# A decoder block on one core: the accounts of the last experts and the final sums

## The chip, the cores and the metric

One core of one Trainium2 chip. The metric is the device time of one execution in microseconds (us); the times given are medians of several runs. The engines are named as in the profile: PE is TensorE, ACT ScalarE, DVE VectorE, POOL GpSimd, SP SyncE (here it only issues DMAs). DMAs issued by SP are made by hardware; the indirect ones that gather and scatter rows by index are issued by GpSimd, which writes their descriptors itself.

## The reference

A decoder block on 512 tokens of 1024 channels in float32: a Mamba-2 mixer and a pooling mixer, merged; then a mixture of 64 experts (256 hidden channels each, 8 of them for each token) and one shared expert; then a final norm. The change lies in the last part:

```python
u2 = modulate(rmsnorm(h, norm_ffn_g), sh2, sc2)
h = h + g2 * moe_ffn(u2, ...)      # routed experts, each weighted, plus the shared expert
return rmsnorm(h, final_norm_g)    # h * rsqrt(mean(h*h) + eps) * g
```

## The kernel before

Tokens lie in four tiles of 128 partitions by 1024 channels (`NT` = 4, `t` counts them). The mixers come first; this document only needs the loop over experts in `experts` and the function `finish`.

The experts run one after the other, in an order written out by hand (`manual_schedule`). For expert `e` the kernel gathers its tokens' rows (a gather on GpSimd), multiplies them by the gate and up weights, forms the hidden product, and multiplies by the down weights. Experts of up to 64 tokens take a light way through PE in float32; others a heavy one, in which ACT and DVE split each weight tile into two parts first. The iteration of `e` runs the down product of `e - 1`, and then the scatter of `e - 1`: GpSimd adds the weighted output rows into one of two accounts in DRAM, `Y[0]` or `Y[1]` (512 x 1024 each, an accumulating indirect DMA). Before the change even experts go to `Y[0]` and odd ones to `Y[1]`, so that two scatters that follow each other need not wait for each other; scatters into the same account do. `Y[0]` starts as the shared expert's output and `Y[1]` as zeros. The number of rows in a scatter is chosen by Ifs on the expert's count (`first`); tokens over 128 go in a second one (`second`). An If's other arm counts up the semaphores that its DMAs would have counted.

Weights come by DMAs on SP's queue, in order, into a ring of eight tiles of 128 x 2048 named `raw`, three for each expert; a load waits until the tile's last reader is done. Behind the last expert's weights SP loads, into tiles of the same ring, the residual `hs2` (two pairs of token tiles, `L1324`), the two rows `k.rows` (the gate g2 and the final norm's weights, broadcast to all partitions, `L1093`, `L1094`), and then `part`, the two pairs of token tiles of `Y[0]` (`L1324` again; both use `token_pair`). For the last expert (63, heavy) the down product and its scatter stand behind the loop. Behind them `part` is multiplied by g2 (`L1290`) and added to `hs2` (`L1291`), tiles 0 and 2 on DVE, 1 and 3 on GpSimd.

`rare_blocks` is an If that is not taken here (an expert with over 256 tokens). `finish` reads the four tiles of `Y[1]` into the tiles of `part` (`L1350`, variable `acc`), multiplies by g2 (`L1345`), adds the sum of before (`L1346`; tile 1 on GpSimd, the others on DVE), squares on ACT with a sum over the row (`L1336`), forms the inverse root on GpSimd in two operations on 128 x 1 (`rsqrt_mean`, `L68` and `L69`), multiplies by the norm's weights on DVE (`L1340`), scales by the root on ACT (`L1341`) and stores (`L1342`).

Of the kernel before, what the change touches and what calls it, by code (L numbers as in the profile page):

```python
# [16 lines left out]
ALU = mybir.AluOpType  # L17
# [6 lines left out]
NT = 4  # L24
# [1018 lines left out]
def scatter(k, idx, b, y, acc, n=P):  # L1043
    k.nc.gpsimd.indirect_dma_start(out=k.Y[acc], out_offset=bass.IndirectOffsetOnAxis(ap=idx[0][:n, b:b + 1], axis=0), in_=y[:n],  # L1044
                                   in_offset=None, bounds_check=T - 1, oob_is_err=False, compute_op=ALU.add)
# [29 lines left out]
def experts(k, shared):  # L1075
# [35 lines left out]
    def sized(n, rows, move):  # L1111
# [6 lines left out]
        with some.Else():  # L1118
            sized(n, rows[mid:], move)

    def first(e, move):
        sized(count(e), (16, 32, 48, 64, 80, 96, 112, P), move)

# [106 lines left out]
    with tc.manual_schedule():  # L1230
        fetch_over(0)
        fetch_over(1)
        if_two(0, lambda: turn(k, k.xg[3], k.xT[1]))
        for e in range(E):
            fetch(e + 2)
            fetch_over(e + 2)
            onehot(e + 4)
            for i in (e, e + 1):
                if i < E:
                    for engines in (every, both):  # L1240
                        count(i, engines)
            if_heavy(e + 1, both, lambda: gu[e + 1][0].split(k, k.gu0w[(e + 1) % 2]))
            hid = products(e)
            hid1, halves = hidden(k), turn_tiles(k)
            slots = slot_tile(k, 2) if e + 4 < E else None

            def turns():
                if e + 1 < E:
                    turn_in(k, xg[e + 1], halves)

            def second_products():
                gate_act(k, gate_up_mm(k, k.xT[(e + 1) % 2], gu[e]), hid1)
                turns()

            def index_part(b):
                if e + 4 < E:
                    slot_product(k, slots, oh[e + 4], k.V[:, :, e + 4, :], b)

            def next_second():
                index_part(0)  # L1260
                turn(k, k.xg[3 + (e + 1) % 2], k.xT[e % 2])

            def second_down():
                ps = turn_tiles(k)[0].rearrange("p q t -> p (q t)")[:, :2 * P].rearrange("p (j t) -> p j t", j=2)
                hidden_in(k, hid1, ps)
                index_part(1)
                hidden_out(k, ps, k.hx[2])
                for n in range(2):
                    down(k, k.hx[2], dn[e], n, k.xg[2], idx[e][1][:, 1:2])

            if_two(e, second_products, turns)
            turned(e + 1, halves)
            if_two(e + 1, next_second, lambda: index_part(0))
            downs(e - 1)
            hidden_turned(e, hid)
            if_two(e, second_down, lambda: index_part(1))
            if e > 0:
                first(e - 1, lambda n: scatter(k, idx[e - 1], 0, k.yl[(e - 1) % 2], (e - 1) % 2, n))
            second(e, lambda n: scatter(k, idx[e], 1, k.xg[2], e % 2, n))
            load(e + 2)  # L1280
            if e + 4 < E:
                idx[e + 4] = slot_numbers(k, slots, 2)
        e = E - 1
        downs(e)
        first(e, lambda n: scatter(k, idx[e], 0, k.yl[e % 2], 1, n))
        part = k.part = [token_pair(k, k.Y[0], t) for t in (0, 2)]
        for t in range(NT):
            eng = (nc.vector, nc.gpsimd)[t % 2]
            y, h = (u[t // 2][:, t % 2, :] for u in (part, k.hs2))
            eng.tensor_mul(y, y, k.rows[:, 0, :])  # L1290
            eng.tensor_add(h, h, y)  # L1291


def rare_blocks(k):
# [33 lines left out]
def finish(k, out):  # L1328
    nc = k.nc
    ys = k.part  # L1330
    ss = k.wp.tile([P, NT], F32, name="oss")
    inv = k.wp.tile([P, NT], F32, name="oinv")
    acc = [ys[t // 2][:, t % 2, :] for t in range(NT)]

    def square(t):
        nc.scalar.activation(k.xg[t], acc[t], AF.Square, accum_out=ss[:, t:t + 1])  # L1336
        rsqrt_mean(k, inv[:, t:t + 1], ss[:, t:t + 1], D)

    def store(t):
        nc.vector.tensor_mul(acc[t], acc[t], k.rows[:, 1, :])  # L1340
        nc.scalar.activation(k.xg[t], acc[t], AF.Copy, scale=inv[:, t:t + 1])  # L1341
        nc.sync.dma_start(out[0, t * P:(t + 1) * P, :], k.xg[t])  # L1342

    def scaled(t, eng):
        eng.tensor_mul(acc[t], acc[t], k.rows[:, 0, :])  # L1345
        eng.tensor_add(acc[t], acc[t], k.hs2[t // 2][:, t % 2, :])  # L1346

    with k.tc.manual_schedule():
        for t in range(NT):
            nc.sync.dma_start(acc[t], k.Y[1][t * P:(t + 1) * P, :])  # L1350
        scaled(0, nc.vector)
        scaled(1, nc.gpsimd)
        square(0)
        scaled(2, nc.vector)
        square(2)
        store(0)
        scaled(3, nc.vector)
        square(1)
        square(3)
        for t in (2, 1, 3):  # L1360
            store(t)


@with_exitstack
# [110 lines left out]
```

## Time and profile before

| | |
|---|---|
| median of 3 runs | 1675.88 us (1669.54 to 1677.01) |
| profiled execution | 1673.0 us |
| its span | 1671.3 us |
| busy: PE, DVE, ACT, POOL | 1475.4, 1011.8, 745.2, 370.3 us |
| last output of expert 63 written by ACT | at 1627.7 us |
| last store issued | at 1663.5 us |

The profile is one execution; its times are us from the start of the span. A row of a timeline gives the start, the duration, the engine, the line of the kernel and the operation as output<-inputs, and in brackets how long the engine was idle before it and what ended that. The engines run side by side, so busy shares don't add up; what counts for the end is the chain of work that ended last. Numbers behind tile names are left out: `raw` can be any tile of the ring.

### The profile page before, as it was taken

How to read it: one execution, taken by the hardware profiler on the slowest of the kernel's cores; microseconds unless marked ns; L12 is line 12 of the kernel's file. 1: busy time of each engine (PE TensorE's matmuls, PEld its weight loads, DVE VectorE, ACT ScalarE, POOL GpSimd, SP SyncE). 2: the span in 40 equal slices, each digit the busy share in tenths (PEclk: the TensorE clock that was granted, in tenths of full speed). 3: DMA queues.
4: the chain of work that ended last, by engine and by line, in shares of the span. 5: the costliest groups of instructions: out<-in, count | busy, mean ns of one | idle time of the engine just before them, and what ended most of it. 6: DMA issues, size and time to landing. Idle time of an engine off the chain costs nothing. (4 is left out here: it accounts for less than half of the span.)

```text
span 1671.3 us, 25992 instructions
## 1 busy us (share of the span) xinstructions
PE 1475.4 (88%) x8084; PEld 1156.2 (69%) x8084; DVE 1011.8 (61%) x1744; ACT 745.2 (45%) x1027; POOL 370.3 (22%) x312
## 2 busy tenths in 40 slices
PE   5999999999999999999898888898798888887970
PEld 5888788788888778888675666566576665665640
DVE  6889778778877974558743354545436453355326
ACT  3465546454434223325544455444536454355332
POOL 5201101002010111220122322322324222221226
PEclk7999999999999999999999999899899989898995
DMA  9442433243333236236738778958889999898974
GB/s 288 122 126 76 138 102 121 76 126 101 107 105 117 82 114 233 87 115 227 294 113 285 252 235 289 329 189 258 282 251 313 324 329 318 287 325 273 297 288 151
DMA packets 152127, 340.32 MB, mean 204 GB/s; under 512 B 15816, under 2 KB 94832, under 8 KB 142272
## 3 DMA queue, kind: packets, MB, share of 16 engines
q1 hardware_dynamic: 135888, 294.94, 51.8%
q0 software_dynamic: 15408, 40.23, 9.4%
q8 instruction: 118, 1.93, 0.5%
q10 hardware_dynamic: 576, 2.10, 0.3%
q14 instruction: 137, 1.12, 0.2%
HBM read 314.00 MB, written 31.01 MB: 206 GB/s over the span
## 5 line engine op out<-in xcount | busy, mean ns | idle before, releaser
L46 DVE TENSOR_TENSOR wl<-raw,wh 128x2048 fp32r<-128x2048 f32 x114 | 273.5, 2404 | 100.0 <-ACT wh L45 88.4
L45 ACT CAST wh<-raw 128x2048 fp32r<-128x2048 f32 x114 | 216.6, 1906 | 140.3 <-PE mm L62 65.7
L1044 POOL DMA_INDIRECT Y<-yl,idx x64 | 108.2, 1691 | 481.8 <-ACT yl L988 271.9
L61 PE MATMUL mm<-uh,wh 128*128 128x512 f32 x432 | 171.7, 397 | 1.9 <-ACT zs L285 1.9
L63 PE MATMUL mm<-uh,wl 128*128 128x512 f32 x432 | 170.4, 395 | 0.0
L62 PE MATMUL mm<-ul,wh 128*128 128x512 f32 x432 | 169.8, 393 | 0.0
L899 PE MATMUL xt<-ident,xg 128*128 128x128 f32 x632 | 97.2, 300 | 58.2 <-issue 18.6
L899 PEld LDWEIGHTS xt<-ident,xg 128*128 128x128 f32 x632 | 84.9, 196 | 77.7 <-issue 48.9
L976 PE MATMUL gu<-raw,xf 128*64 128x256 f32 x1056 | 125.9, 387 | 6.1 <-DMA raw<-in_we_up_dram 3.5
L885 POOL DMA_INDIRECT xg<-u2d,idx x75 | 93.5, 1247 | 117.5 <-DVE oh L851 36.4
L46 DVE TENSOR_TENSOR pair<-raw,pair 128x2048 fp32r<-128x2048 f32 x33 | 75.0, 2290 | 58.2 <-ACT pair L45 49.7
L976 PEld LDWEIGHTS gu<-raw,xf 128*64 128x64 f32 x1056 | 77.2, 138 | 42.6 <-issue 7.2
L61 PE MATMUL gu<-wh,xh 128*128 128x512 f32 x256 | 103.1, 403 | 1.0 <-ACT xh L909 0.6
L62 PE MATMUL gu<-wl,xh 128*128 128x512 f32 x256 | 101.9, 398 | 0.7 <-DVEq L1169 0.7
L63 PE MATMUL gu<-wh,xl 128*128 128x512 f32 x256 | 101.3, 396 | 0.0
L1226 DVE TENSOR_TENSOR hT<-hT,ht 128x128 f32<-128x128 f32 x33 | 9.5, 288 | 146.8 <-ACTq L1169 142.5
L61 PEld LDWEIGHTS mm<-uh,wh 128*128 128x128 f32 x432 | 81.6, 189 | 20.4 <-ACT zs L285 2.3
L63 PEld LDWEIGHTS mm<-uh,wl 128*128 128x128 f32 x432 | 81.6, 189 | 17.7 <-issue 0.9
L62 PEld LDWEIGHTS mm<-ul,wh 128*128 128x128 f32 x432 | 81.5, 189 | 16.8 <-issue 0.4
L45 ACT CAST pair<-raw 128x2048 fp32r<-128x2048 f32 x33 | 62.1, 1903 | 61.7 <-DMA raw<-in_we_gate_dram 22.8
L985 PE MATMUL yo<-raw,hT 128*64 128x512 f32 x264 | 75.5, 695 | 3.5 <-DMA raw<-in_we_gate_dram 2.0
L327 DVE SCALAR_TENSOR_TENSOR cv<-mm,cw,cv 128x511 f32<-128x511 f32 (+2 forms) x90 | 66.6, 741 | 2.1 <-ACT cv L324 1.8
(354 smaller groups left out, 3336.8 us busy)
## 6 DMA issues: line engine op xcount, KB each, us to landing
raw<-in_we_gate_dram SPq DMA_DIRECT2D x124, 512.0 KB
raw<-in_we_up_dram SPq DMA_DIRECT2D x124, 512.0 KB
raw<-in_we_down_dram SPq DMA_DIRECT2D x62, 1024.0 KB
raw<-in_w_in_dram SPq DMA_DIRECT2D x27, 1024.0 KB
raw<-in_w_ada_dram SPq DMA_DIRECT2D x16, 1024.0 KB
big<-in_w_ada_dram SPq DMA_DIRECT2D x16, 512.0 KB
raw<-in_w_in_dram SPq DMA_DIRECT2D x16, 512.0 KB
raw<-in_w_br_ssd_dram SPq DMA_DIRECT2D x8, 1024.0 KB
```

The lines of the kernel that those rows point to most:

```text
L45: nc.scalar.copy(h, raw)
L46: nc.vector.tensor_sub(l, raw, h.bitcast(F32))
L61: nc.tensor.matmul(out, sh, mh, start=first, stop=False)
L62: nc.tensor.matmul(out, sh, ml, start=False, stop=False)
L63: nc.tensor.matmul(out, sl, mh, start=False, stop=last)
L327: nc.vector.scalar_tensor_tensor(cv[:, sft:], ps[:, :T - sft], k.cw[:, j * 32 + blk:j * 32 + blk + 1], cv[:, sft:], op0=ALU.mult, op1=ALU.add)
L885: k.nc.gpsimd.indirect_dma_start(out=xg[:n], out_offset=None, in_=k.u2d, bounds_check=T - 1, oob_is_err=False, in_offset=bass.IndirectOffs ...
L899: k.nc.tensor.transpose(pv[:, q, :], xv[:, hf * 4 + q, :], k.ident)
L976: nc.tensor.matmul(ps[s * LIGHT:(s + 1) * LIGHT, :256], x[:, kk, :], w[:, s, kk % 4, :], start=kk == 0, stop=kk == NK - 1)
L985: nc.tensor.matmul(ps[n * LIGHT:(n + 1) * LIGHT, :], x[:, j, :], unit.raw[:, j * D + n * 512:j * D + n * 512 + 512], start=j == 0, stop=j ...
L1044: k.nc.gpsimd.indirect_dma_start(out=k.Y[acc], out_offset=bass.IndirectOffsetOnAxis(ap=idx[0][:n, b:b + 1], axis=0), in_=y[:n], in_offset= ...
L1226: nc.vector.tensor_mul(k.hT, k.hT, ps[:, :, LIGHT:])
```

## The change

1. A function `account` gives the account of an expert: the last two experts (62 and 63) add to `Y[1]`, all others as before. 62 moves from `Y[0]` to `Y[1]`; with 61 that makes the last three experts that share one account.
2. The reads of `part` and its eight operations move into the last iteration of the loop, ahead of the down product and the scatter of expert 63, and all eight run on DVE.
3. In `finish` all multiplications and additions run on DVE, tiles in the order 0 to 3, and the norm's weights and the root are applied by one `scalar_tensor_tensor` on DVE in place of a multiplication on DVE and a scaling on ACT.

```diff
+    def account(e):
+
+        return 1 if e > E - 3 else e % 2
...
             if e > 0:
-                first(e - 1, lambda n: scatter(k, idx[e - 1], 0, k.yl[(e - 1) % 2], (e - 1) % 2, n))
-            second(e, lambda n: scatter(k, idx[e], 1, k.xg[2], e % 2, n))
+                first(e - 1, lambda n: scatter(k, idx[e - 1], 0, k.yl[(e - 1) % 2], account(e - 1), n))
+            second(e, lambda n: scatter(k, idx[e], 1, k.xg[2], account(e), n))
             load(e + 2)
             if e + 4 < E:
                 idx[e + 4] = slot_numbers(k, slots, 2)
-        e = E - 1
+            if e == E - 1:
+                part = k.part = [token_pair(k, k.Y[0], t) for t in (0, 2)]
+                for t in range(NT):
+                    y, h = (u[t // 2][:, t % 2, :] for u in (part, k.hs2))
+                    nc.vector.tensor_mul(y, y, k.rows[:, 0, :])
+                    nc.vector.tensor_add(h, h, y)
         downs(e)
         first(e, lambda n: scatter(k, idx[e], 0, k.yl[e % 2], 1, n))
-        part = k.part = [token_pair(k, k.Y[0], t) for t in (0, 2)]
-        for t in range(NT):
-            eng = (nc.vector, nc.gpsimd)[t % 2]
-            y, h = (u[t // 2][:, t % 2, :] for u in (part, k.hs2))
-            eng.tensor_mul(y, y, k.rows[:, 0, :])
-            eng.tensor_add(h, h, y)
...
-    def square(t):
+    def scaled(t):
+        nc.vector.tensor_mul(acc[t], acc[t], k.rows[:, 0, :])
+        nc.vector.tensor_add(acc[t], acc[t], k.hs2[t // 2][:, t % 2, :])
         nc.scalar.activation(k.xg[t], acc[t], AF.Square, accum_out=ss[:, t:t + 1])
         rsqrt_mean(k, inv[:, t:t + 1], ss[:, t:t + 1], D)
 
     def store(t):
-        nc.vector.tensor_mul(acc[t], acc[t], k.rows[:, 1, :])
-        nc.scalar.activation(k.xg[t], acc[t], AF.Copy, scale=inv[:, t:t + 1])
+        o = inv[:, t:t + 1]
+        nc.vector.scalar_tensor_tensor(k.xg[t], acc[t], o, k.rows[:, 1, :], op0=ALU.mult, op1=ALU.mult)
         nc.sync.dma_start(out[0, t * P:(t + 1) * P, :], k.xg[t])
-
-    def scaled(t, eng):
-        eng.tensor_mul(acc[t], acc[t], k.rows[:, 0, :])
-        eng.tensor_add(acc[t], acc[t], k.hs2[t // 2][:, t % 2, :])
...
-        scaled(0, nc.vector)
-        scaled(1, nc.gpsimd)
-        square(0)
-        scaled(2, nc.vector)
-        square(2)
-        store(0)
-        scaled(3, nc.vector)
-        square(1)
-        square(3)
-        for t in (2, 1, 3):
-            store(t)
+        for t in range(NT):
+            scaled(t)
+            if t > 1:
+                store(t - 2)
+        store(NT - 2)
+        store(NT - 1)
```

The order of SP's queue from the load of the rows on, before the change (`raw_6053` is `k.rows`, `raw_6166` and `raw_6167` are the two tiles of `part`; the branches belong to Ifs of the last iteration and of the last down product and scatter):

```order
L1093 DMA raw_6053<-modrow_57 128x1024
L1094 DMA raw_6053<-in_final_norm_g_dram 128x1024
L1169 UNCONDITIONAL_BRANCH
L1160 UNCONDITIONAL_BRANCH x2
L1116 UNCONDITIONAL_BRANCH
L1169 UNCONDITIONAL_BRANCH
L1126 UNCONDITIONAL_BRANCH
L1160 UNCONDITIONAL_BRANCH
L1324 DMA raw_6166<-Y0_60 128x2x1024
L1116 UNCONDITIONAL_BRANCH
L1324 DMA raw_6167<-Y0_60 128x2x1024
```

and after it:

```order
L1093 DMA raw_6053<-modrow_57 128x1024
L1094 DMA raw_6053<-in_final_norm_g_dram 128x1024
L1130 UNCONDITIONAL_BRANCH
L1327 DMA raw_6166<-Y0_60 128x2x1024
L1173 UNCONDITIONAL_BRANCH
L1164 UNCONDITIONAL_BRANCH x2
L1327 DMA raw_6167<-Y0_60 128x2x1024
L1116 UNCONDITIONAL_BRANCH
L1173 UNCONDITIONAL_BRANCH
L1130 UNCONDITIONAL_BRANCH
L1164 UNCONDITIONAL_BRANCH
```

The two reads of `Y[0]` have moved ahead of the branches of the last down product and scatter; nothing else on the queue has moved.

The order of DVE from the end of expert 63's hidden product, before the change (`raw_6747` and `raw_6748` are the tiles of `hs2`; rows of the rare blocks are left out at the dots):

```order
L1015 TENSOR_TENSOR hl2_6177<-xt_25467,hh2_6176 128x256
L1169 UNCONDITIONAL_BRANCH x2
...
L1290 TENSOR_TENSOR raw_6166<-raw_6166,raw_6053 128x1024
L1297 TENSOR_LOAD rare_6458
...
L1291 TENSOR_TENSOR raw_6747<-raw_6747,raw_6166 128x1024
L1290 TENSOR_TENSOR raw_6167<-raw_6167,raw_6053 128x1024
L1291 TENSOR_TENSOR raw_6748<-raw_6748,raw_6167 128x1024
L1345 TENSOR_TENSOR raw_6166<-raw_6166,raw_6053 128x1024
L1346 TENSOR_TENSOR raw_6166<-raw_6166,raw_6747 128x1024
```

and after it:

```order
L1015 TENSOR_TENSOR hl2_6177<-xt_25467,hh2_6176 128x256
L1173 UNCONDITIONAL_BRANCH x2
L1291 TENSOR_TENSOR raw_6166<-raw_6166,raw_6053 128x1024
L1292 TENSOR_TENSOR raw_6747<-raw_6747,raw_6166 128x1024
...
L1164 COMPARE_AND_BRANCH
L1164 UNCONDITIONAL_BRANCH x2
L1116 UNCONDITIONAL_BRANCH
L1300 TENSOR_LOAD rare_6458
...
L1339 TENSOR_TENSOR raw_6166<-raw_6166,raw_6053 128x1024
L1340 TENSOR_TENSOR raw_6166<-raw_6166,raw_6747 128x1024
```

The eight operations on `part` (two shown) stand between the hidden product of expert 63 and the branches of its down product (`L1164`) and scatter (`L1116`), and the final sums follow behind the rare blocks.

## Rows read from the trace of the kernel before

**Rows 1.** The page's first part: the span, and the busy time of each engine with its share and its instructions.

```profile
span 1671.3 us, 25992 instructions
PE 1475.4 (88%) x8084; PEld 1156.2 (69%) x8084; DVE 1011.8 (61%) x1744; ACT 745.2 (45%) x1027; POOL 370.3 (22%) x312
```

**Rows 2.** The chain of waits that ended last, from 1628 us on: start, duration, what it was.

```profile
1628.02 8.47 DMA Y<-yl,idx
...
1636.73 2.07 another core or an unknown queue
...
1646.98 3.30 POOL raw L1345
...
1659.49 1.41 POOL oinv L69
...
1662.35 1.15 ACT xg L1341
```

**Rows 3.** The timeline of SP's queue in the last 70 us: start, duration of the issue (of several: from the first to the last), line, DMA.

```profile
1605.40 3.62 SPq L1324 DMA_DIRECT2D raw<-hsd  x2
1609.11 0.42 SPq L1093 DMA_DIRECT2D raw<-modrow  x1
1609.62 0.38 SPq L1094 DMA_DIRECT2D raw<-in_final_norm_g_dram  x1
1626.85 0.88 SPq L1324 DMA_DIRECT2D raw<-Y  x2
1638.89 8.43 SPq L1350 DMA_DIRECT2D raw<-Y  x4
```

**Rows 4.** What SP's queue waited for from 1590 us on: us in total, times, longest.

```profile
SPq L1324 <- DMA Y<-yl,idx: 16.7, 1, 16.7
```

**Rows 5.** The timeline of POOL: the scatters of experts 60 to 63 (`L1044`, the time in which GpSimd writes the descriptors), a multiplication of the final sums, and one pair of the tiny operations.

```profile
1597.54 1.33 POOL L1044 DMA_INDIRECT Y<-yl,idx  x1 [3.69 <-ACT yl L988]
1613.88 2.41 POOL L1044 DMA_INDIRECT Y<-yl,idx  x1 [15.01 <-ACT yl L988]
1623.71 1.29 POOL L1044 DMA_INDIRECT Y<-yl,idx  x1 [7.42 <-ACT yl L988]
1628.02 1.44 POOL L1044 DMA_INDIRECT Y<-yl,idx  x1 [3.02 <-ACTq L1298]
...
1646.94 3.32 POOL L1345 TENSOR_TENSOR raw<-raw 128x1024 f32<-128x1024 f32 x1
...
1658.72 0.69 POOL L68 TENSOR_SCALAR oinv<-oss 128x1 f32<-128x1 f32 x1
1659.49 1.41 POOL L69 TENSOR_TENSOR oinv<-oinv,mhalf 128x1 f32<-128x1 f32 x1
```

**Rows 6.** The timeline of DVE from expert 63's weights to the final sums.

```profile
1612.83 2.28 DVE L46 TENSOR_TENSOR wl<-raw,wh 128x2048 fp32r<-128x2048 f32 x1
...
1623.87 0.43 DVE L1015 TENSOR_TENSOR hl<-ht,hh 128x256 fp32r<-128x256 f32 x1 [3.61 <-ACTq L1169]
1631.90 1.22 DVE L1290 TENSOR_TENSOR raw<-raw 128x1024 f32<-128x1024 f32 x1 [7.61 <-DMA raw<-Y]
...
1642.07 2.71 DVE L1345 TENSOR_TENSOR raw<-raw 128x1024 f32<-128x1024 f32 x1 [2.93 <-DMA raw<-Y]
1644.82 3.24 DVE L1346 TENSOR_TENSOR raw<-raw 128x1024 f32<-128x1024 f32 x1
...
1657.00 1.23 DVE L1346 TENSOR_TENSOR raw<-raw 128x1024 f32<-128x1024 f32 x1
```

**Rows 7.** The instruction of POOL's queue that counts up DMA semaphores in an If's arm, first in the If of the rare blocks (`L1298`), then in those of the second scatters (`L1126`, from 1500 to 1640 us): durations in ns (least, median, longest), first and last start.

```profile
L1298 POOLq INC_SWDGE_SEM  x1: 2132/2132/2132, 1636.8 to 1636.8; - x1
...
L1126 POOLq INC_SWDGE_SEM  x18: 1702/1917/2087, 1502.1 to 1623.8; - x18
```

**Rows 8.** Stretches of the end: from and to, length, busy time of PE, PEld, DVE, ACT and POOL (with instructions), the granted clock, the busy share of the DMA engines, GB/s.

```profile
1604.00:1616.00 12.00, 8.28 (x31) 5.26 (x30) 6.07 (x5) 8.35 (x9) 2.12 (x1) 0.81 1.02 410
...
1624.00:1627.00 3.00, 2.96 (x12) 2.07 (x12) 0.29 (x1) 0.69 (x1) 1.00 (x1) 1.00 0.10 14
1627.00:1636.00 9.00, 0.00 (x0) 0.00 (x0) 3.88 (x2) 0.69 (x1) 4.83 (x2) 0.61 0.88 276
...
1629.00:1630.00 1.00, 0.00 (x0) 0.00 (x0) 0.00 (x0) 0.00 (x0) 0.46 (x1) 0.51 1.01 418
```

**Rows 9.** The timelines of PE and ACT: PE's last reader of expert 62's down weights, ACT's last output of expert 63, and the end of a square in `finish`.

```profile
1620.08 1.94 PE L985 MATMUL yo<-raw,hT 128*64 128x512 f32 x8 [0.75 <-ACTq L1169]
...
1627.06 0.69 ACT L1040 ACTIVATE yl<-yo,wt 128x512 f32<-128x512 f32 x1 [0.69 <-PEq L1298]
...
1658.24 0.19 ACT L1336 ACTIVATION_READ_ACCUMULATOR xg<-raw 128x1 f32 x1
```

**Rows 10.** Single lines of the kernel: durations in ns (least, median, longest), first and last start, shape. `L692` is the norm ahead of the experts.

```profile
L692 DVE SCALAR_TENSOR_TENSOR xg<-hs,inv,a x4: 1277/1278/1279, 751.1 to 762.9; 128x1024 f32<-128x1024 f32 x4
...
L69 POOL TENSOR_TENSOR oinv<-oinv,mhalf x4: 549/1426/1607, 1654.8 to 1661.8; 128x1 f32<-128x1 f32 x4
...
L1336 ACT ACTIVATE xg<-raw x4: 1040/1048/1057, 1648.1 to 1658.3; 128x1024 f32<-128x1024 f32 x4
...
L1342 SPq DMA_DIRECT2D out_dram<-xg x4: 332/336/338, 1657.4 to 1663.5; - x4
```

**Rows 11.** The scatters of the whole kernel (`L1044`): the time from issue to landing, where the trace shows it.

```profile
DMA to landing us min/median/max: 3.6/6.2/8.8
```

## Prediction

> **What bounds the kernel now.** I read the shares of the engines first [rows 1]: TensorE is busy for 88% of the span, but the change touches none of that work. It touches the end, so the view to read is the chain of waits that ended last, from the last expert on [rows 2], and beside it what the DMA queue of SyncE, GpSimd, VectorE, ScalarE and the DMA engines did there [rows 3 to 9].
>
> The end runs so. ScalarE writes the last expert's output at 1627.06 + 0.69 = 1627.75 [rows 9]; GpSimd issues its scatter at 1628.02 [rows 5]. The scatter lands 8.47 us later, at 1636.49 [rows 2]. Behind it GpSimd passes the If around the rare blocks, where an instruction that counts up its DMA semaphores takes 2.13 us [rows 7], and SyncE waits for it: its first read of `Y[1]` goes out at 1638.89 [rows 3], 2.4 us behind the landing. VectorE starts on that tile at 1642.07 [rows 6], 3.2 us later. From there to the last store at 1663.5 [rows 10] GpSimd is on the chain with a whole share of the sums and then four pairs of tiny operations. From the last store to the end of the span 7.8 us pass, which the change doesn't touch.
>
> Two things in this end are self-made. The reads of `Y[0]` go out at 1626.85, after a wait of 16.7 us for the scatter of expert 62 [rows 3, 4], so 2 MB of reads run beside the last scatter. And VectorE and GpSimd slow each other: the same 128x1024 operation takes VectorE 1.22 or 1.23 us in some rows and 2.71 and 3.24 in others, which lie beside GpSimd's 3.32 [rows 5, 6].
>
> **The change part by part.**
>
> *Accounts.* Expert 62 adds to `Y[1]`, not `Y[0]`, so `Y[0]` is complete with expert 60's scatter, issued at 1597.54 [rows 5]; with the 8.8 us of the slowest landing [rows 11] it is there by 1606.4. The price is a wait: the scatters of 61, 62 and 63 now follow each other into one account. 61 is issued at 1613.88 and by 8.8 us lands by 1622.7, before 62's 1623.71. 62 landed 3.1 us after its issue (1626.85, when SyncE's wait for it ended [rows 3 to 5]), 0.9 before 63's output is ready. Now a read of 1 MB lies beside it; I take 63's start as 1628.2 instead of 1628.0, and up to 1628.6.
>
> *Reads of `Y[0]`.* Two DMAs of 1 MB move on SyncE's queue, from behind the expert's end to behind the rows at 1609.62 [rows 3]. The first needs the buffer of 62's gate and up weights, free by then, and goes at about 1610. Its bytes come behind what saturates the DMA engines until 1616 [rows 8], so it delays no weight ahead of it, and has landed long before 1624. The second needs the buffer of 62's down weights, which PE reads until 1620.08 + 1.94 = 1622.0 [rows 9]; with the 5.05 us of the first pair before (1626.85 to 1631.90 [rows 3, 6]) it lands near 1627.1. Behind it SyncE has only the reads of `Y[1]`, which wait for longer anyway.
>
> *Early sums.* Eight operations on VectorE, behind its last split of the hidden product at 1623.87 + 0.43 = 1624.3 [rows 6]. At 1.23 us each they end by 1624.3 + 9.8 = 1634.1. PE and ScalarE wait in expert 63 for VectorE's earlier products alone, so nothing stands behind the sums but the final ones. Their cover is the flight of the last scatter and the 2.4 + 3.2 us behind it: cost nothing. Without that cover, if they came after it as now, they would cost their share again.
>
> *The last scatter.* It has 276 GB/s x 9 us = 2.48 MB in its stretch [rows 8] less 2 x 1.05 MB of reads = 0.39 MB to itself. Alone it should take what 62's small one took, 3.1, and the time of its bytes: 0.9 us at the 418 GB/s of the best microsecond, 1.6 at some 250 GB/s. Nearest row above: 8.47 with the reads beside it. Then there is the descriptor writing on GpSimd: 1.29 and 1.44 us with VectorE idle, 2.41 beside VectorE's 2.28 us subtraction [rows 5, 6], and the early sums now lie beside it. I add 0.8 for that: 3.1 + 1.6 + 0.8 = 5.5 us, nearer to the free rows than to 8.47 since the reads are gone; ends 4.0 and 8.5.
> The Trainium skill (SBUF — State Buffer, section Who interferes with whom) says that an operation of VectorE with two SBUF inputs contends with a GpSimd instruction that reads SBUF, but infers that it leaves descriptor writing alone. By that rule the 0.8 would be nothing and the gain below 0.8 larger; the 2.41 us row speaks against it.
>
> *Reads of `Y[1]`.* They keep their place. All four can go at once, because no GpSimd sum holds a buffer: with VectorE's early sums done at 1634.1 they go from 1628.2 + 5.5 + 2.4 = 1636.1 on, and the first tile is there 3.2 us later, at 1639.3. The others follow at 512 KB in 1.3 to 1.9 us (410 and 276 GB/s [rows 8]), faster than VectorE's 2.46 us for a tile.
>
> *Final sums on VectorE alone.* Until the last tile is summed: 8 x 1.23 for the sums and one 1.28 for the first store, since the combined operation has the shape of the first norm's [rows 10]: 11.1 us, to 1650.4. Nothing large is left on GpSimd, so I take the undisturbed durations. Then the last tile's square and its accumulator read on ScalarE, 1.04 + 0.19; GpSimd's two tiny operations with their gaps, 0.3 + 0.69 + 0.08 + 1.0 ([rows 5, 9, 10]; the second has rows from 0.55, with VectorE idle, to 1.61; here VectorE ends two stores during it); the combined operation, 1.28; gaps 0.2. That is 4.8 us, to 1655.2. ScalarE's 1.15 us scaling is gone from it.
>
> **The sum.** 1655.2 + 7.8 = 1663.0 against 1671.3: 8.3 us less. Of these 2.8 come from the scatter, and 5.5 from the final sums. The profiled execution took 1673.0, so it would take 1664.7. The three runs lie at 1669.5, 1675.9 and 1677.0; with the profiled one their mean is 1673.9, 2 us under the median. From it the forecast is 1665.6, and I give **1666**.
>
> Bounds of the gain: with a start at 1628.0, a landing after 4.0, 2.0 instead of 2.4 (the semaphore instruction has rows from 1.70 [rows 7]) and 0.55 for the last tiny operation the end is 1660.4, 10.9 less. With 1628.6, 8.5 and 1.61 it is 1667.0, 4.3 less.
>
> **The rivals.**
>
> *The scatter stays slow.* It lands after 8.5 us even without the reads, or waits for 62's landing that much longer, because the three scatters share an account and VectorE holds up their descriptors. For it: landings up to 8.8 us [rows 11]. Against it: these stand in streams of weights, and the engines moved 14 GB/s in the 3 us before this scatter [rows 8]. Then only the final sums gain: about 4.3 to 5.5 us, near 1669.
>
> *The scatter is early.* Descriptors are written in the 1.44 us of the free rows although VectorE works beside, and the bytes go at 418 GB/s. By the bounds: 10.9 less, near 1663. For it: both are rows. Against it: the 2.41. The page of the Trainium skill cited above would have the descriptors so.
>
> *Slower: VectorE's long durations are not GpSimd's doing.* If the 3.24 us come from the DMA writing the same tiles, or from the adds themselves, they stay, and ten such operations of VectorE alone now lie on the path (eight for the sums, two combined): 1639.3 + 9 x 3.24 + 3.5 + 3.24 + 7.8 = 1683.0, 11.7 more, near 1685. It is slower than before from 2.1 us an operation on, and measurably so from 2.9. Against it: 1.22 at 1631.90 in the stretch with the reads at 276 GB/s, and 1.23 at 1657.00, for a multiply and an add [rows 6, 8].
>
> *The early sums don't come early.* If the second read lands late and they end at 1638 instead of 1634.1, nothing is lost: VectorE reaches the fourth tile of `Y[1]` only at 1639.3 + 7.4 + 1.3 = 1648, so its read may wait until 1643. This rival has no price and no chance of its own.
>
> **How the numbers follow.** A measurement of this kernel can tell about 0.5% from no change, 8.4 us: faster is below 1667.5. The forecast, a gain of 6.5 to 9.5, gets 0.60; the slow scatter 0.22; the early one 0.14; slower 0.04. The forecast's 8.3 us lie just at the bound from the mean of the runs, but 2 us beyond it from their median: of it I count 0.40 as faster and 0.20 as same; the early scatter is faster, 0.14; of the slow one 0.03 is faster. That makes 0.57 faster, 0.39 same, 0.04 slower. The range takes in gains from 4.3 to 10.9 about 1673.9, which is 1663.0 to 1669.6, and 2 to 3 us on either side for the spread of the runs: 1660 to 1672.
>
> **What would show it.** SyncE's reads of `Y[0]` at about 1610 and 1622; eight VectorE operations of 1.2 us between 1624 and 1634.5; the last scatter's landing 4 to 6.5 us after an issue at 1628 to 1628.6 (all against the same point of expert 63); four reads of `Y[1]` close together; VectorE's final operations at 1.2 to 1.3 us; some 16 us from the first of these to the last store. The forecast is wrong if the scatter still takes over 7.5 us, if VectorE's rows stay above 2 us, or if 62's landing holds up 63 by more than 1 us.

## The result, and the profile after

| | median | runs |
|---|---|---|
| before | 1673.44 us | 6, 1669.54 to 1677.01 |
| after | 1662.99 us | 6, 1659.15 to 1669.2 |

The ratio is 0.994, with a 95% interval from 0.9915 to 0.9966: faster, by about what the prediction said could just be told. Measured again beside more runs (below, `after_again`) it is 0.9974 [0.9961, 0.9987]. The two say how coarse a median is here. What tells the mechanism is the end of each profile (its last 36 to 44 us), and I measure it from one point in all of them: from the moment when ScalarE has written the last output of expert 63 (its last `L1040`) to the end of the span. Before, that is 1671.3 - 1627.75 = 43.55 us [rows 1, 9].

The profiled execution of after took 1669.2 us. The first part of its page; beside [rows 1] GpSimd lost 18 us of work, and VectorE has six instructions more and nearly the same busy time:

```profile
span 1667.5 us, 25982 instructions
PE 1475.2 (88%) x8084; PEld 1157.4 (69%) x8084; DVE 1009.2 (61%) x1750; ACT 741.1 (44%) x1023; POOL 352.5 (21%) x306
```

ACT's timeline, the last output of expert 63:

```profile
1631.07 0.69 ACT L1040 ACTIVATE yl<-yo,wt 128x512 f32<-128x512 f32 x1 [0.69 <-PEq L1301]
```

So this end starts at 1631.76 and lasts 1667.5 - 1631.76 = 35.74 us: **7.8 us less** than before, where the sum said 8.3. (All times of after are thus some 4 us later than those of before at the same point of the program.)

The timeline of SP's queue at the end; `L1327` holds the two reads of `Y[0]`, `L1351` those of `Y[1]`:

```profile
1615.30 11.16 SPq L1327 DMA_DIRECT2D raw<-Y  x2
1641.32 1.77 SPq L1351 DMA_DIRECT2D raw<-Y  x4
1653.09 7.12 SPq L1347 DMA_DIRECT2D out_dram<-xg  x4
```

The first two reads went out at 1615.30 and 1626.1 (the row runs to the end of the second issue), instead of together behind a scatter; the four others go within 1.77 us where they took 8.43 [rows 3]. The first of those stands 9.56 us behind ScalarE's output, before 1638.89 - 1627.75 = 11.14.

POOL's timeline, the scatters of 61, 62 and 63 and the last tiny operation:

```profile
1617.15 2.41 POOL L1044 DMA_INDIRECT Y<-yl,idx  x1 [15.01 <-ACT yl L988]
1627.72 1.29 POOL L1044 DMA_INDIRECT Y<-yl,idx  x1 [8.16 <-ACT yl L988]
1632.70 2.20 POOL L1044 DMA_INDIRECT Y<-yl,idx  x1 [3.69 <-DVE raw L1291]
...
1657.98 0.55 POOL L69 TENSOR_TENSOR oinv<-oinv,mhalf 128x1 f32<-128x1 f32 x1
```

63's scatter begins 0.94 us behind the output (before 0.27), and its descriptors take 2.20 us (before 1.44) [rows 5]. The name in the last bracket, an early sum, misleads: the wait is for 62's landing. That is seen in the queue's own semaphore waits on that line and, in the second row, in the instruction that counts up the DMA semaphores in the If of the rare blocks (durations in ns, first and last start):

```profile
L1044 POOLq EVENT_SEMAPHORE  x2: 17/597/1177, 1630.4 to 1630.5; - x2
...
L1301 POOLq INC_SWDGE_SEM  x1: 2132/2132/2132, 1639.2 to 1639.2; - x1
```

GpSimd's queue waited from 1630.5 for 1.18 us, to 1631.7, which is 3.9 us behind 62's issue; then it passes the Ifs that choose the number of rows, and issues 63's scatter 1.0 us later. The second row starts where 63's scatter has landed, at most 6.5 us after its issue (before 8.47 [rows 2], with this instruction 0.3 us later [rows 7]), and SP's read comes 2.1 us behind the instruction's start, as before [rows 3, 7].

DVE's timeline: the first early sum, the two around 63's descriptors, the last one; then the first final one, a combined operation, and the last:

```profile
1628.71 1.23 DVE L1291 TENSOR_TENSOR raw<-raw 128x1024 f32<-128x1024 f32 x1 [0.41 <-DVEq L1173]
...
1632.36 1.22 DVE L1292 TENSOR_TENSOR raw<-raw 128x1024 f32<-128x1024 f32 x1
1633.51 1.22 DVE L1291 TENSOR_TENSOR raw<-raw 128x1024 f32<-128x1024 f32 x1
...
1637.15 1.22 DVE L1292 TENSOR_TENSOR raw<-raw 128x1024 f32<-128x1024 f32 x1
1644.59 1.23 DVE L1339 TENSOR_TENSOR raw<-raw 128x1024 f32<-128x1024 f32 x1 [6.21 <-DMA raw<-Y]
...
1651.78 1.28 DVE L1346 SCALAR_TENSOR_TENSOR xg<-raw,oinv 128x1024 f32<-128x1024 f32 x1
...
1658.56 1.28 DVE L1346 SCALAR_TENSOR_TENSOR xg<-raw,oinv 128x1024 f32<-128x1024 f32 x1 [0.71 <-POOL oinv L69]
```

No long rows are left: 1.22 to 1.28 us where [rows 6] had 2.71 and 3.24. The early sums lie under the scatter and are over at 1638.4; VectorE then sits idle for 6.2 us until `Y[1]` is there. From the first final operation to the last store (the line below: durations in ns, first and last start) 15.3 us pass; before 1663.5 - 1642.07 = 21.4 [rows 6, 10].

```profile
L1347 SPq DMA_DIRECT2D out_dram<-xg x4: 332/335/338, 1653.1 to 1659.9; - x4
```

Two stretches in the form of [rows 8], the first beside the second read of `Y[0]`, the second with the scatter's bytes alone:

```profile
1629.00:1630.00 1.00, 1.00 (x6) 0.83 (x5) 0.96 (x2) 0.32 (x1) 0.01 (x1) 1.00 1.02 422
...
1635.40:1638.60 3.20, 0.00 (x0) 0.00 (x0) 2.94 (x3) 0.00 (x0) 0.00 (x0) 0.50 0.82 117
```

The DMA queues during the last scatter (packets, MB, share of the 16 DMA engines; `q0` has the scatter's bytes, `q1` the reads): first before, from 1628.1 to 1632.9 and from 1632.9 to 1636.2, then after, from 1635.4 to 1638.6:

```profile
q1 hardware_dynamic: 419, 1.65, 94.2%
...
q0 software_dynamic: 112, 0.37, 56.9%
q1 hardware_dynamic: 117, 0.42, 34.2%
...
q0 software_dynamic: 112, 0.37, 82.3%
```

Before, the scatter's first packet moves only at 1632.9, 3.45 us behind the end of its descriptors (1628.02 + 1.44); after, 0.57 us behind it. Once it moves, its 0.37 MB take 3.2 us before and 3.1 after.

### The profile page after: what moved, and what is told of

It is laid out like the page before. It is cut to its first block, busy times and chain, and to the rows that moved or that the text cites. A ratio compares the mean times of both kernels' runs of the same rounds, so it can differ in the third digit from the quotient of the medians.

```text
span 1667.5 us, 25982 instructions
## 1 busy us (share of the span) xinstructions
PE 1475.2 (88%) x8084; PEld 1157.4 (69%) x8084; DVE 1009.2 (61%) x1750; ACT 741.1 (44%) x1023; POOL 352.5 (21%) x306
## 3 DMA queue, kind: packets, MB, share of 16 engines
q14 instruction: 137, 1.12, 0.2%
## 5 line engine op out<-in xcount | busy, mean ns | idle before, releaser
L1044 POOL DMA_INDIRECT Y<-yl,idx x64 | 109.4, 1710 | 486.2 <-ACT yl L988 278.1
L899 PE MATMUL xt<-ident,xg 128*128 128x128 f32 x632 | 95.8, 297 | 55.8 <-ACT wh L45 18.7
```

The source lines that it names most:

```text
L899: k.nc.tensor.transpose(pv[:, q, :], xv[:, hf * 4 + q, :], k.ident)
```

## The experiments

The table has all of them, with the kernels before and after, as seen in one profile each. Its columns (us): the issue of 63's scatter behind ScalarE's last output; the writing of its descriptors; the first read of `Y[1]` behind that output; from there to the issue of the last store; and the whole end. From the last store to the end of the span 7.6 to 7.8 us remain in all. Kernels for which no median is told were run once, so their profiles alone are used.

| kernel | issue | descriptors | first read | to last store | end |
|---|---|---|---|---|---|
| before | 0.27 | 1.44 | 11.14 | 24.6 | 43.55 |
| after | 0.94 | 2.20 | 9.56 | 18.6 | 35.74 |
| after_again | 0.75 | 2.40 | 9.44 | 18.5 | 35.58 |
| e1_finish_only | 0.27 | 1.44 | 11.14 | 22.0 | 40.76 |
| e2_early_only | 0.83 | 2.32 | 9.65 | 21.1 | 38.45 |
| e3_parity | 0.27 | 1.44 | 11.13 | 18.6 | 37.29 |
| e4_no_early_sums | 0.92 | 1.44 | 8.47 | 18.6 | 34.71 |
| e5_own_account | 0.28 | 1.63 | 8.10 | 18.5 | 34.22 |
| e6_pool_tile | 0.94 | 2.22 | 9.56 | 23.4 | 40.51 |
| e7_mul_act | 1.39 | 1.76 | 9.30 | 19.2 | 36.17 |
| e8_no_rare | 0.54 | 1.44 | 5.95 | 18.6 | 32.11 |
| e10_early_reads | 0.28 | 1.61 | 8.03 | 18.4 | 34.16 |
| e11_half_sums | 0.96 | 1.44 | 8.68 | 18.6 | 34.94 |
| e12_wide_adds | 0.70 | 2.30 | 9.45 | 18.7 | 35.72 |

### after_again: the kernel after, once more

> The changed kernel once more, to see how far its end repeats. The end is counted from the moment ACT has written the last output of expert 63 to the end of the span: 43.5 us before, 35.7 us in the first profile of the changed kernel. If the gain sits in the end, the end repeats within 0.5 us while the time ahead of it scatters by some us, and the ratio to the kernel before is 0.993 to 0.996. If the time ahead of the end has changed too, the point at which expert 63 is done is lower than before on the median, and the ratio is 0.992 or less.

End 35.58, 0.16 from the first profile. The median was 1667.76 us against 1671.86 (12 and 29 runs), ratio 0.9974 [0.9961, 0.9987], outside the expected 0.993 to 0.996. The end repeats to a few tenths, the median doesn't: a gain of 7.8 us is 0.47% of 1673, and this interval lies below it, the first one's middle above. In the 14 profiles the scatter of expert 60, which stands ahead of everything that the change touches, starts anywhere between 1594.4 us (`e10`) and 1602.4 us (`e4`). Why this series of runs kept only 4.1 of the 7.8 us, no run here shows.

### e1 and e2: each half of the change alone

`e1_finish_only` is the kernel before with the new `finish`, `e2_early_only` the kernel after with the old one:

```diff
-        nc.vector.tensor_mul(acc[t], acc[t], k.rows[:, 1, :])
-        nc.scalar.activation(k.xg[t], acc[t], AF.Copy, scale=inv[:, t:t + 1])
...
+        nc.vector.scalar_tensor_tensor(k.xg[t], acc[t], o, k.rows[:, 1, :], op0=ALU.mult, op1=ALU.mult)
...
-        scaled(0, nc.vector)
-        scaled(1, nc.gpsimd)
...
+        for t in range(NT):
+            scaled(t)
+            if t > 1:
+                store(t - 2)
...
```

That is `e1` against before; `e2` against after is the same piece the other way round.

> The kernel before with the new final sums alone; accounts, reads of the first account and early sums as before. My theory, that the two parts lean on each other: GpSimd still holds tiles 1 and 3 of the first account's sums until some 19 us into the end, the read of tile 3 waits for that, and VectorE is slowed meanwhile, so the end is 40 to 41.5 us, 2 to 3.5 less than before, and the ratio 0.998. Rival, that the final sums on VectorE alone carry the gain: the end is 36 to 37.5 us, ratio 0.996.

> The changed kernel with the old final sums (tile 1 on GpSimd, multiplication on VectorE, scaling on ACT); accounts and early sums as changed. My theory: GpSimd is free when the second account arrives and starts its tile 4 us sooner than before, the read goes out 1.6 us sooner, and the end is 37.5 to 39 us, 4.5 to 6 less than before, ratio 0.997. Rival, that accounts and early sums bring little because the gain is in the new final sums: the end is 41 to 43 us, ratio 0.999 to 1.

Ends 40.76 and 38.45: 2.79 and 5.10 us less than before, and 2.79 + 5.10 = 7.9 is the whole gain of 7.8. Both ends lie where their theory had them. But since they add up, the halves don't lean on each other in the total, as the expectation of `e1` has it: the new `finish` is worth 2.79 us without the early sums and 38.45 - 35.74 = 2.71 with them. In `e1` the timelines of DVE and POOL show why the new `finish` alone gives so little:

```profile
1642.07 2.60 DVE L1336 TENSOR_TENSOR raw<-raw 128x1024 f32<-128x1024 f32 x1 [3.10 <-DMA raw<-Y]
1644.70 3.25 DVE L1337 TENSOR_TENSOR raw<-raw 128x1024 f32<-128x1024 f32 x1
...
1643.67 3.20 POOL L1291 TENSOR_TENSOR raw<-raw 128x1024 f32<-128x1024 f32 x1
```

GpSimd's share of the sums over `Y[0]` still runs beside VectorE's first final operations. In `e2` the same happens with tile 1 of the final sums:

```profile
1648.21 3.25 DVE L1349 TENSOR_TENSOR raw<-raw 128x1024 f32<-128x1024 f32 x1
...
1647.17 3.20 POOL L1349 TENSOR_TENSOR raw<-raw 128x1024 f32<-128x1024 f32 x1
```

Their medians are 1672.74 (12 runs, of which one took 2850.44 us; 1671.16 without it; ratio 1.0004 [0.9981, 1.0028]) and 1669.39 us (0.9978 [0.9966, 0.9991]); the first alone can't be told from no change.

### e3: the account by parity again

```diff
     def account(e):
-        return 1 if e > E - 3 else e % 2
+        return e % 2
```

> The changed kernel with the old accounts, expert 62 into the first one. The reads of that account then wait for expert 62's scatter again and lie beside the last scatter. My theory: the last scatter takes 8 to 9 us from its issue, the sums of tiles 2 and 3 end some 14 us into the end, and the end is 37 to 38.5 us, 1.5 to 2.5 more than the changed kernel. Rival, that the account doesn't matter because the wait for expert 62 in the same account eats what the reads give: the end is 35.5 to 36.5 us.

End 37.29, as the theory said. Timelines of POOL and SP:

```profile
1630.18 1.44 POOL L1044 DMA_INDIRECT Y<-yl,idx  x1 [3.03 <-ACTq L1301]
...
1629.01 0.88 SPq L1327 DMA_DIRECT2D raw<-Y  x2
1641.04 3.01 SPq L1351 DMA_DIRECT2D raw<-Y  x4
```

The reads of `Y[0]` wait for 62 again and lie beside the last scatter, and the first read of `Y[1]` is at 11.13 us, as before. So the account is worth 37.29 - 35.74 = 1.55 us of the 7.8, and the rest doesn't need it: even here VectorE is done with the early sums when the first tile of `Y[1]` comes. The median, 1665.25 us (0.9957 [0.994, 0.9974]), is *lower* than that of the kernel after in the same series, 1667.76, though the end is longer. The two intervals overlap, so the medians don't order these two kernels: in the 14 profiles ScalarE's last output ends between 1625.4 us (`e10`) and 1633.3 us (`e4`), in kernels that are nearly the same up to there.

### e4: no early sums

```diff
-                for t in range(NT):
-                    y, h = (u[t // 2][:, t % 2, :] for u in (part, k.hs2))
-                    nc.vector.tensor_mul(y, y, k.rows[:, 0, :])
-                    nc.vector.tensor_add(h, h, y)
```

> The changed kernel without the eight early operations; the first account is read and not added, so its share is left out of the output. My theory, that VectorE beside it slows the descriptor writing of the last scatter: the last scatter's descriptors take 1.4 to 1.5 us instead of 2.20, it lands 0.7 to 0.9 us sooner after its issue, and the end is 34.7 to 35.2 us. Rival, that descriptor writing doesn't depend on VectorE and 2.20 us has another cause: 2.2 us, end 35.5 to 36.

End 34.71, the theory's lower edge; POOL's timeline has

```profile
1634.21 1.44 POOL L1044 DMA_INDIRECT Y<-yl,idx  x1 [3.67 <-ACTq L1297]
```

1.44 us instead of 2.20, at an issue as late as in the kernel after (0.92 and 0.94). So the early sums, costed at nothing but for the descriptors, cost up to 1.0 us, 0.8 of them in the descriptors. The other 0.3 lies in the flight of the scatter's bytes, 2.9 us against 3.1, which differs as much between kernels that have the early sums (2.9 to 3.2), so one profile doesn't show it to be theirs. The late issue isn't theirs.

### e5: an account of its own for expert 62

```diff
...
-        return 1 if e > E - 3 else e % 2
+        return 2 if e == E - 2 else 1 if e > E - 3 else e % 2
...
```

(at the dots, the third account `Y[2]` is made and zeroed).

> The changed kernel with expert 62 adding to a third account that nobody reads, so its share is left out of the output. The last scatter then waits for nothing but its data and expert 61's scatter. My theory, that the scatter of expert 62 lands late beside the second read of the first account and holds up the last one: the last scatter is issued 0.2 to 0.4 us after ACT's last output instead of 0.94, end 35.0 to 35.3 us. Rival, that GpSimd is held up by VectorE's early sums or by its branches: it stays at 0.8 to 1.0 us, end 35.7.

POOL's and SP's timelines:

```profile
1626.36 1.63 POOL L1045 DMA_INDIRECT Y<-yl,idx  x1 [3.00 <-ACTq L1302]
...
1634.18 1.77 SPq L1352 DMA_DIRECT2D raw<-Y  x4
```

The issue came as the theory said, 0.28 behind the output. The end, 34.22, is 1.5 shorter and not the expected 0.4 to 0.7: the descriptors were shorter too (1.63 for 2.20), which neither side foresaw.

### e6: one tile of the final sums back on GpSimd

```diff
+        eng = nc.gpsimd if t == 1 else nc.vector
-        nc.vector.tensor_mul(acc[t], acc[t], k.rows[:, 0, :])
+        eng.tensor_mul(acc[t], acc[t], k.rows[:, 0, :])
```

(and the addition likewise).

> The changed kernel with the final multiplication and addition of tile 1 on GpSimd, all else as changed. My theory, that the two engines slow each other: VectorE's operations beside it take 2.7 to 3.4 us, and from the first of the final operations to the last store pass 17 to 18.5 us instead of 15.3; end 37.5 to 39. Rival, that a second engine takes work off the path: VectorE has two operations less, 13 us, end 33.5.

The end is 40.51, worse than the theory's 37.5 to 39 and far from the rival's 33.5. DVE's and POOL's timelines:

```profile
1645.47 3.38 DVE L1347 SCALAR_TENSOR_TENSOR xg<-raw,oinv 128x1024 f32<-128x1024 f32 x1 [0.47 <-POOL oinv L69]
1648.77 3.35 DVE L1340 TENSOR_TENSOR raw<-raw 128x1024 f32<-128x1024 f32 x1
...
1645.43 2.33 POOL L1340 TENSOR_TENSOR raw<-raw 128x1024 f32<-128x1024 f32 x1
1647.84 3.20 POOL L1341 TENSOR_TENSOR raw<-raw 128x1024 f32<-128x1024 f32 x1
```

The combined operation, 1.28 us alone, takes 3.38 beside GpSimd. And the roots of three tiles now queue behind GpSimd's addition, which the theory had left out. This is the clearest case against the slower rival: VectorE's long rows come and go with GpSimd's work beside them.

### e7: the norm's weights and the root apart again

```diff
-        nc.vector.scalar_tensor_tensor(k.xg[t], acc[t], o, k.rows[:, 1, :], op0=ALU.mult, op1=ALU.mult)
+        nc.vector.tensor_mul(acc[t], acc[t], k.rows[:, 1, :])
+        nc.scalar.activation(k.xg[t], acc[t], AF.Copy, scale=o)
```

> The changed kernel with the norm's weights multiplied on VectorE and the root applied by a scaling on ACT, as before, in place of the combined operation. My theory: VectorE's multiplication takes as long as the combined operation and can be done while GpSimd forms the root, so only ACT's 1.15 us stands behind the last root instead of 1.28 on VectorE; end within 0.3 us of 35.7. Rival, that the combined operation saves a step on the path: end 36.5 to 37 us.

End 36.17, 0.4 more than after: above the theory's band and below the rival's, so neither. ACT's timeline has the last scaling

```profile
1654.49 1.15 ACT L1347 ACTIVATE xg<-raw,oinv 128x1024 f32<-128x1024 f32 x1 [0.33 <-POOL oinv L69]
```

From the first final operation (1639.85) to the last store (1655.7) it takes 15.9 us, after 15.3: the one operation is worth some 0.55 us here, and part of that is hidden in the end by an earlier first read (0.26). The late issue in this row of the table (1.39) is 62's landing: GpSimd's wait for it ended 4.4 us behind its issue, where the eight other kernels with the second read beside 62 and one account for both show 3.5 to 4.0.

### e8: without the If of the rare blocks

```diff
         experts(k, shared)
-        rare_blocks(k)
         finish(k, out)
```

> The kernel after without the two-way branch and the extra blocks for experts of many rows that stand between the last scatter and the final reads (no expert of these inputs enters the branch). The end is counted from ScalarE's last output of expert 63 to the end of the span: 35.7 us after. Theory: the semaphore instruction of 2.13 us on GpSimd's queue behind the branch stands on the path, and the first read of the last account comes 1.9 to 2.4 us sooner after the scatter's last bytes: end 33.3 to 33.9. Rival: the read waits for the scatter's own landing, which the profile shows no row for, and the semaphore instruction runs beside that wait: end 35.2 to 35.8, the first read 9.2 to 9.6 us after the output as it was.

Even more than the theory: end 32.11, 3.6 us less. The chain of waits that ended last has

```profile
1628.83 5.27 DMA Y<-yl,idx
...
1634.24 3.25 DMA raw<-Y
```

The scatter lands at 1634.10 and the read goes out 0.14 us behind it; before, 2.4 us passed there, from 1636.49 to 1638.89 [rows 2, 3]. Counted from the scatter's last packet it is 0.46 us here and 2.7 in eleven of the other kernels (2.9 in `e1` and `e3`). So the If and its semaphore instruction are worth **2.2 to 2.3 us on the path**, as the theory had it. The rest of the 3.6 us is an earlier issue (0.4), shorter descriptors (0.8) and a flight of the bytes that is 0.2 shorter.

### e10: the second pair of `Y[0]` read early

```diff
-                part = k.part = [token_pair(k, k.Y[0], t) for t in (0, 2)]
+                part = token_pair(k, k.Y[0], 0)
+                k.part = [part[:, 0, :], part[:, 1, :], k.xg[0], k.xg[1]]
+                for t in (2, 3):
+                    nc.sync.dma_start(k.part[t], k.Y[0][t * P:(t + 1) * P, :])
...
```

(at the dots, the operations on these tiles take their new names, and `finish` writes squares and results into the tiles of `hs2`).

> The kernel after with the first account's tiles 2 and 3 read early, beside tiles 0 and 1 (into the row tiles, since the buffer that the kernel after reads them into is not free before expert 62 is done), and with squares and results put into the shared-expert tiles. Theory: expert 62's scatter landed late because the second read moved beside it; now it moves alone, expert 63's scatter is issued 0.2 to 0.4 us after ScalarE's last output (kernel after: 0.94), with descriptors still at 1.6 to 2.4 us beside VectorE; end 34.8 to 35.3 us against 35.7 and a ratio to the kernel before of 0.994 to 0.997. Rival: a scatter into the account that the next one adds to takes its 4.9 us from issue to release whatever moves beside it; issue at 0.75 to 0.95, end 35.5 to 35.9.

The theory holds: issue at 0.28, end 34.16 (0.6 under its band, again by shorter descriptors), and the lowest ratio to before in the study, 1660.72 us against 1673.71 (6 and 10 runs), 0.9924 [0.9898, 0.995]. POOL's timeline, and the semaphore waits of its queue on that line:

```profile
1625.72 1.61 POOL L1044 DMA_INDIRECT Y<-yl,idx  x1 [3.03 <-ACTq L1304]
```

```profile
L1044 POOLq EVENT_SEMAPHORE  x2: 17/153/289, 1624.1 to 1624.2; - x2
```

62 was issued at 1621.40 and had landed when the wait ended, at 1624.2 + 0.29 = 1624.5: 3.1 us, against 3.9 in the kernel after with the read beside it (3.5 to 4.4 in the nine kernels that have the read there and wait for 62). It is the start of 62's bytes that the read holds up: the first packet moves 0.57 us behind the descriptors here and 1.30 in the kernel after.

### e11 and e12: early sums of half and of double length

```diff
-                    nc.vector.tensor_mul(y, y, k.rows[:, 0, :])
-                    nc.vector.tensor_add(h, h, y)
+                    for s in (slice(0, D // 2), slice(D // 2, D)):
+                        nc.vector.tensor_mul(y[:, s], y[:, s], k.rows[:, 0, s])
+                        nc.vector.tensor_add(h[:, s], h[:, s], y[:, s])
```

in `e11`, and in `e12`:

```diff
...
-                    nc.vector.tensor_add(h, h, y)
+                for i in range(2):
+                    nc.vector.tensor_add(k.hs2[i], k.hs2[i], part[i])
```

> The kernel after with each of the eight early sums cut into two operations on 128x512, which should take some 0.6 to 0.7 us each. In the eight profiles so far whose early sums run on VectorE while expert 63's descriptors are written, the writing took 1.44 to 2.40 us and ended 0.14 to 0.24 us after the start of one of VectorE's operations. Theory: the writing ends only where VectorE goes from one operation to the next; with boundaries every 0.6 to 0.7 us it takes 1.44 to 2.1 us and again ends 0.1 to 0.25 us behind a start. Rival: VectorE slows the writing by sharing a port in proportion to its busy time, wherever its operations begin: 2.2 to 2.4 us as in most of the profiles, the end at any distance from a start.

> The kernel after with the early sums as four products on 128x1024 and then two additions on 128x2048, which should take some 2.4 us each; expert 63's descriptors are written while the first addition runs. Theory: the writing ends where that addition ends, 3.0 to 3.7 us after it began, 0.1 to 0.25 us behind the start of the second addition; the end of the span, counted from ScalarE's last output, grows to 36.5 to 37.2 us. Rival: sharing in proportion to busy time: 2.2 to 2.4 us, the end 35.5 to 36.0.

In `e11` (DVE's and POOL's timelines) the descriptors took 1.44 us:

```profile
1631.80 0.74 DVE L1292 TENSOR_TENSOR raw<-raw 128x512 f32<-128x512 f32 x1
...
1631.82 1.44 POOL L1044 DMA_INDIRECT Y<-yl,idx  x1 [3.71 <-DVE raw L1292]
```

in `e12` 2.30:

```profile
1629.35 1.22 DVE L1291 TENSOR_TENSOR raw<-raw 128x1024 f32<-128x1024 f32 x1
1630.48 2.28 DVE L1293 TENSOR_TENSOR raw<-raw 128x2048 f32<-128x2048 f32 x1
...
1629.58 2.30 POOL L1044 DMA_INDIRECT Y<-yl,idx  x1 [3.44 <-DVE raw L1291]
```

`e11` speaks against the rival (1.44, not 2.2 to 2.4), `e12` against the theory, though the rival's numbers fit it: the writing ended at 1631.88, in the middle of the long addition, after 2.30 us and not 3.0 to 3.7. So the theory as stated falls, and the rival too. What fits both, and the others, is a wait at the *beginning*; it is shown in the last section.

## Why the prediction was right, point by point

The time (1662.99 for 1666, in the range) and the direction held, and so did the mechanism; the sum of 8.3 us was 0.5 too large, since two terms were off in opposite directions.

- **Scatter, forecast 2.8 us, measured 1.6** (first read of `Y[1]` at 9.56 against 11.14 us). This is the term that was mis-sized. Its start was taken 0.2 us later than before, and at most 0.6; it was 0.67 later, which is 0.5 of the 1.2 that are missing. The bound had 62 landed 0.9 us ahead of 63's output, by the 3.1 us of before [rows 3 to 5]; `e10` shows that 3.1 again, and the kernel after shows 3.9 with the second read beside it. I had seen the read beside it, but not that the wait for 62 stands ahead of the Ifs in GpSimd's queue, which take another 1.0 us. `e5` and `e10` take the delay away in two ways. The other 0.7 is its duration: I took 5.5 us, and it was at most 6.5 to the semaphore instruction behind the landing, some 6.2 counted as before. The bytes went at 117 GB/s for 3.1 us, where I had added 0.9 to 1.6 us for them at 250 to 418 GB/s. What the reads had cost this scatter before was its start, not its pace: its bytes took 3.2 us then too, but began 3.45 us behind the descriptors instead of 0.57.
- **Descriptors, 0.8 us**: 2.20 - 1.44 = 0.76, and gone in `e4`. That VectorE holds them up is right; the size is luck, since other kernels with early sums paid 0 to 0.96 (last section).
- **2.4 us from landing to read**: 2.4 were taken as untouched, and they were; `e8` shows that all but 0.14 of them are the If.
- **Reads of `Y[0]`**: forecast at about 1610 and 1622, which is 1614 and 1626 in the times of after; 1615.3 and 1626.1. Right. The first was indeed not on anybody's path.
- **Early sums at no cost**: 1628.71 to 1638.4, 0.3 to 0.4 us later than forecast and under cover; their price, 0.8 us by `e4`, is that of the descriptors, which the sum has in the scatter's term.
- **Final sums, forecast 5.5 us, measured 6.1** (from VectorE's first final operation to the last store, 21.4 to 15.3; forecast 15.9). The 0.6 between are small: the pairs of sums follow each other every 2.40 us (1.22 and 1.23, overlapping by some 0.05), where I had 2.46, and the last tile's way has shorter gaps. Its two tiny operations took 1.12 + 0.55 us for the 0.69 + 1.0 of the sum. Only part of the 6.1 is the new `finish`: in `e2`, with the old one, the stretch from the first read to the last store already fell from 24.6 to 21.1 us.
- **The rivals.** The slow scatter and the early one lie on either side of what came. Both causes that the slow one named were real, 62's landing (0.67 us) and the descriptors (0.76), but its landing after 8.5 us did not come. The slower one, VectorE's long rows without GpSimd, is refuted by the rows of 1.22 to 1.28 us, and by `e6` the other way round.
- **The chances.** The gain lies at the bound of 0.5%: one measurement beyond it, one within. 0.57 and 0.39 was a fair split, and on which side a measurement falls is luck.

## What to carry to other kernels

Where a kernel's end is a chain, measure it from one event in each profile: the end repeated to 0.2 us in two profiles while the medians lay almost 5 us apart, and its terms added up (2.79 + 5.10 for 7.8). An accumulating scatter into the account of the one before waits for that one's landing, and a 1 MB read beside the earlier scatter lengthened that wait from 3.1 us to between 3.5 and 4.4; put reads where no scatter is in flight. And splitting float32 work on two SBUF operands between VectorE and GpSimd gave a loss here: one tile of the final sums on GpSimd made the end 4.8 us longer (`e6`), with operations of VectorE up to 2.7 times as long. An untaken If behind an indirect DMA cost 2.2 to 2.3 us at the place where nothing covered it.

## What was not expected of the hardware

**The descriptors of an indirect DMA wait for the operation that VectorE is in.** Without VectorE beside it the writing of 63's descriptors took 1.44 us (before, `e1`, `e3`, `e4`); beside it 1.44 to 2.40. In eight profiles it ended 1.31 us after the end of the VectorE operation that was running when it began: in the kernel after at 1632.36 + 1.22 + 1.31 = 1634.89 (1632.70 + 2.20 = 1634.90 by its own row), in `e12` at 1629.35 + 1.22 + 1.31 = 1631.88, and likewise in `after_again`, `e2`, `e5`, `e6`, `e7` and `e10`. In `e8` that operation had 0.03 us left, and the writing took its 1.44. In `e11` the writing began within 0.02 us of an operation's start, again took 1.44, and that operation took 0.74 us instead of the 0.69 of its neighbours: there VectorE seems to have waited. So the price is what is left of the running operation when the writing begins, less 0.12 us: 0 to 0.96 us here, and luck decides.

This reading was formed on 63's scatter after the runs, and earlier scatters of the same profiles bear it out. One falls beside VectorE's subtraction of a weight split, at another point of it in each profile. In `e4`, then in `e12`:

```profile
1484.54 2.28 DVE L46 TENSOR_TENSOR wl<-raw,wh 128x2048 fp32r<-128x2048 f32 x1
1484.99 3.01 POOL L1044 DMA_INDIRECT Y<-yl,idx  x1 [6.52 <-ACT yl L988]
...
1483.02 2.29 DVE L46 TENSOR_TENSOR wl<-raw,wh 128x2048 fp32r<-128x2048 f32 x1
1484.88 1.61 POOL L1044 DMA_INDIRECT Y<-yl,idx  x1 [8.12 <-ACT yl L988]
```

The same descriptors take 3.01 and 1.61 us, and in all 14 profiles they end 1.19 us after the end of the subtraction. Five other scatters that fall beside such a subtraction do the same: 0.42 to 1.82 us of it were left when they began, and each ends at a distance of its own behind it, between 1.18 and 1.37 us, which is the same to 0.01 us in all 14 profiles. So does 61's, whose 2.41 us the prediction used: 1.18 behind the subtraction [rows 5, 6].

The Trainium skill (SBUF — State Buffer, section Who interferes with whom) describes such a lock, in which whoever comes first has the shared ports for a whole instruction and the other stands still, and the waits above agree with it. But it infers that an operation like VectorE's sums leaves descriptor writing alone; the 2.20 us against 1.44 without them differ from that, and the measurement decides.

**The bytes of the accumulating scatter are slow in themselves, and reads ahead of them hold up their start.** The last scatter moved 0.37 MB at 117 GB/s with the DMA engines at a share of 0.82, while plain reads reached 422 GB/s at 1.02. In all 14 kernels its bytes took 2.9 to 3.2 us, with the reads of `Y[0]` in flight or not. But with them (before, `e1`, `e3`) the first packet moved 3.3 to 3.5 us behind the end of the descriptors, and without them 0.57 us in all eleven. Why the rate is so low, no run here shows.
